# The first MLP product by Strassen's seven block products, and the second in eight banks

## The chip, the cores and the metric

The kernel runs on one core of one Trainium2 chip. The metric is the device time of one execution in microseconds (us), the median over several runs. The engines are named as the profile names them: PE is TensorE (matmuls; PEld its weight loads), DVE VectorE, ACT ScalarE, POOL GpSimd, SP SyncE, which here only issues DMAs. SBUF is the on-chip memory with 128 partitions, PSUM the eight accumulator banks of 512 float32 values per partition, DRAM the memory outside the core.

## The reference

One layer of an encoder on x (512 tokens, 1024 channels, float32). Three branches (a convolution with GLU, differential attention over 8 heads, chunked spatial gating) are projected, gated and summed, and an MLP follows. The MLP is what the change touches:

```python
h = rms_norm(x, norm_ffn_pre[l])
f = jnp.square(jax.nn.relu(h @ w_ffn_up[l]))     # 1024 -> 4096
y = f @ w_ffn_down[l]                            # 4096 -> 1024
x = x + rms_norm(y, norm_ffn_post[l])
```

## The kernel before

All of it is one function, `encoder_layer`. S = 512 is the number of tokens, P = 128 the number of partitions, KT = 8 the channel tiles of the model width, TT = 4 the token tiles, FT = 32 the channel tiles of the MLP's inner width.

**Split products.** Every large matmul runs in float32r. An operand is kept as a high half (a copy on ACT that rounds it) and a low half (a subtraction on DVE), and a product is three matmuls, high by high, high by low, low by high (`mm3`, L227). `unit` (L243) makes one channel tile: 8 contraction tiles by 3, 24 matmuls of 512 moving columns with a 128x128 stationary tile each.

**Weights.** `specs` (L87 to L128) lists all weight blocks of 1024 elements per partition (512 KB) in the order of use. `load_to` (L139) issues a block's DMA on SP into `w_raw`, copies it on ACT to `w_hi` (L150) and subtracts on DVE for `w_lo` (L151); each of the three has three buffers in the pool `wp`, but the last four blocks of the output projection and the MLP's first have their halves in the pool `p4`. `take` (L154) hands out the next blocks and keeps two more under way.

**Order.** A scheduler merges the instructions that the code emits into one order for each engine; PE's matmuls stay in the order of the code. SP, ACT, DVE, PE and POOL each work through their own order, and a buffer that is used again waits for its last reader. A pool that is opened where a closed one lay waits for the readers of that memory in the same way.

**Around the MLP.** The output projection and the second norm (p4, L760 to L814) write x1d to DRAM on SP (L801), and transpose the normed tokens into `h2h` and `h2l` (DVE L224), the MLP's moving operands, held in the pool `hp` in the places of `hh` and `hl`. Since the last tokens come late, the first four channel tiles are begun with their first 256 tokens (L807 to L813) and finished with the second 256 (L819 on): halves of 24 matmuls of 256 columns.

**First product (L817 to L833).** For each of 32 channel tiles 24 matmuls of 512 columns, then Relu (ACT L830), square (DVE L831), high half `fh` (ACT L832) and low half `fl` (DVE L833). Weights are stationary and activations move.

**Second product (L835 to L870).** Here `fh` and `fl` are stationary and the weights move. For each half `nh` of the output's columns, 16 blocks by 4 token tiles by 6 matmuls of 512 into four banks: tag "b" for the first half, "a" for the second. The last 2 or 3 blocks of a half are taken together and done token tile by token tile, with the finish behind each (ACT L860, DVE L861, and for the second half the norm, L869, and the output's DMAs, L870).

Of the kernel before, what the change touches and what calls it, by code (L numbers as in the profile page):

```python
# [40 lines left out]
TURN = {(2, 2): 0, (3, 2): 1, 1: 2, 2: 3}  # L41
W0AT = 1
LOWP = 3000
ZA, ZB, QO, KO, VO, SU, SV, GL = 0, 1024, 2048, 3072, 4096, 5120, 6144, 7168


@with_exitstack
def encoder_layer(ctx: ExitStack, tc: tile.TileContext, a: dict, out: bass.AP):
# [88 lines left out]
    taken = [0]  # L137

    def load_to(n):  # L139
        while len(loaded) < min(n, len(specs)):  # L140
            if len(loaded) in xp["set"] and xp["pool"] is None:
                break
            src = specs[len(loaded)]
            m = src.shape[2]
            raw = wp.tile([P, 1024], F32, tag="raw", bufs=3, name="w_raw")
            p, n_ = (xp["pool"], 5) if len(loaded) in xp["set"] else (wp, 3)
            hi = p.tile([P, 1024], F32R, tag="hi", bufs=n_, name="w_hi")
            lo = p.tile([P, 1024], F32R, tag="lo", bufs=n_, name="w_lo")
            nc.sync.dma_start(raw.rearrange("p (k c) -> p k c", c=m), src)
            act.activation(hi, raw, AF.Copy)  # L150
            vec.tensor_tensor(lo, raw, f32(hi[:, :]), op=ALU.subtract)  # L151
            loaded.append((hi.rearrange("p (k c) -> p k c", c=m), lo.rearrange("p (k c) -> p k c", c=m)))
# [91 lines left out]
        run(unit_gen(b, w, mov))  # L244


    hh = hp.tile([P, KT, S], F32R, tag="hh", name="hh")
    hl = hp.tile([P, KT, S], F32R, tag="hl", name="hl")
    with mk("p0") as p0:
        gpre = p0.tile([P, D], F32, tag="gpre", name="gpre")  # L250
        act.dma_start(gpre, a["norm_mix_pre"].partition_broadcast(P))
# [507 lines left out]

    dp = ctx.enter_context(mk("dp", space=DRAM))  # L760
    x1d = dp.tile([S, D], F32, name="x1d")
    h2h = hp.tile([P, KT, S], F32R, tag="hh", name="h2h")
    h2l = hp.tile([P, KT, S], F32R, tag="hl", name="h2l")
    with mk("p4") as p4:
        xp["pool"] = p4
        gpost = bcast(p4, "gpost", a["norm_mix_post"], D)
# [49 lines left out]

    fp = ctx.enter_context(mk("fp"))  # L817
    gpo = bcast(fp, "gpo", a["norm_ffn_post"], D)
    fh = fp.tile([P, FT, S], F32R, tag="fh", name="fh")  # L819
    fl = fp.tile([P, FT, S], F32R, tag="fl", name="fl")  # L820
    for n in range(FT):
        if n < len(early):
            b = eb[n]
            run(unit_gen(b[:, 256:512], early[n], h2, slice(256, 512)))
        else:
            (w,) = take(1)
            b = bank("a")
            unit(b, w, h2)
        r = fp.tile([P, S], F32, tag="r", bufs=2, name="r")
        act.activation(r, b, AF.Relu)  # L830
        vec.tensor_tensor(r, r, r, op=ALU.mult)  # L831
        act.activation(fh[:, n], r, AF.Copy)  # L832
        vec.tensor_tensor(fl[:, n], r, f32(fh[:, n]), op=ALU.subtract)  # L833

    def down_mm(bs, t, i, w):  # L835
        tk = slice(t * P, (t + 1) * P)
        for k in range(2):
            kt = 2 * i + k
            mm3(bs[t], (fh[:, kt, tk], fl[:, kt, tk]), [x_[:, k] for x_ in w], kt == 0, kt == FT - 1)

    xs = hp.tile([P, TT, D], F32, tag="hh", name="xs")
    us = hp.tile([P, TT, D], F32, tag="hl", name="us")
    pool.dma_start(xs, x1d.rearrange("(t p) c -> p t c", p=P))
    ss = cp.tile([P, TT, 2], F32, tag="fss", name="fss")
    NCH = FT // 2
    es = []
    for nh in range(2):
        bs = [bank("b" if nh == 0 else "a") for _ in range(TT)]
        hf = slice(nh * 512, (nh + 1) * 512)
        tail = 2 + nh  # L850
        for i in range(NCH - tail):
            (w,) = take(1)
            for t in range(TT):
                down_mm(bs, t, i, w)
        ws = take(tail, 1)
        for t in range(TT):
            for i in range(tail):
                down_mm(bs, t, NCH - tail + i, ws[i])
            jk = fp.tile([P, S], F32, tag="r", bufs=2, name="jk")
            act.activation(jk, bs[t], AF.Square, accum_out=ss[:, t, nh:nh + 1])  # L860
            vec.tensor_tensor(us[:, t, hf], bs[t], gpo[:, hf], op=ALU.mult)  # L861
            if nh == 0:
                es.append(eps_with(cp, ss[:, t, 0:1], 1.0 / D))
            else:
                r = rstd_of(cp, ss[:, t, 1:2], 1.0 / D, es[t], es[t])
            if nh:
                for e, i in ((nc.sync, 0), (act, 1)):
                    hf = slice(i * 512, (i + 1) * 512)
                    vec.scalar_tensor_tensor(us[:, t, hf], us[:, t, hf], r, xs[:, t, hf], op0=ALU.mult, op1=ALU.add)  # L869
                    e.dma_start(out[t * P:(t + 1) * P, hf], us[:, t, hf])  # L870
    ph.close()


# [29 lines left out]
```

## Time and profile before

| what | value |
|---|---|
| median of 3 runs | 1090.18 us (1090.12 to 1090.3) |
| the profiled execution's own time | 1090.09 us |
| its span, first to last instruction | 1088.0 us |
| mean granted TensorE clock | 0.997 |
| first product's matmuls, from its first tiles' second token halves on | 740.12 to 906.86 us |
| second product's matmuls | 906.86 to 1080.95 us |
| w_raw's blocks by DMA | 176 of 512 KB |

A row of the chain or the timeline reads: start in us, length in us, engine, line, operation, and output <- inputs. In square brackets stands how long the engine sat idle before it and what ended that. In rows that group instructions, the total of busy time is followed by the mean of one in ns. DVE and ACT overlap the end of an instruction with the start of the next, so the time from one start to the next is what one costs in a row of them. The ends of matmuls are modelled; the distance of their starts is not.

### The profile page before, as it was taken

To read this page: it belongs to the slowest core of one execution; us is meant where nothing else is said; L and a number is where in the kernel's file an instruction comes from. 1 tells how busy PE (TensorE), PEld (TensorE's weight loads), DVE (VectorE), ACT (ScalarE), POOL (GpSimd) and SP (SyncE) were. 2 spreads that over 40 slices of the span, in tenths; PEclk is the share of its full clock that TensorE was granted. 3 is DMA by queue.
4 is the path that set the end of the run, shared out by engine and by line. 5 is a ranking of instruction groups with operands and counts; after the bars stand their busy time and mean duration, and the time that the engine had idled before them with its cause. 6 is when DMAs were issued, how large, how long until landed. Compare 5 with 4: busy or idle time off the path is not lost.

```text
span 1088.0 us, 13538 instructions
## 1 busy us (share of the span) xinstructions
PE 1074.6 (99%) x5232; PEld 904.7 (83%) x5232; DVE 706.2 (65%) x1201; ACT 497.6 (46%) x800; POOL 14.0 (1%) x32
## 2 busy tenths in 40 slices
PE   8999999999999999999999999999999999999997
PEld 7989898988878888888888888889888888888886
DVE  6686878978996888997996554485444443223224
ACT  5356677776654832343222863354444443112111
POOL 3000000000000000000000000000000000000000
PEclk9999999999999999999999999999999999999999
DMA  7242332232333333322333132732333334223222
GB/s 223 78 127 68 96 98 78 78 98 78 93 101 97 97 97 97 97 78 80 98 97 102 52 116 97 277 129 78 97 97 97 97 97 174 97 97 96 97 78 78
DMA packets 149439, 111.78 MB, mean 103 GB/s; under 512 B 3957, under 2 KB 130977, under 8 KB 149376
## 3 DMA queue, kind: packets, MB, share of 16 engines
q1 hardware_dynamic: 146368, 101.73, 31.0%
q0 software_dynamic: 2288, 7.63, 2.0%
q10 hardware_dynamic: 720, 1.57, 0.4%
q8 instruction: 41, 0.67, 0.3%
q14 instruction: 22, 0.18, 0.1%
HBM read 102.52 MB, written 4.19 MB: 98 GB/s over the span
## 4 chain that ended last, share of the span: by engine, by line
PE 94%; DVE 2%; ACT 2%; DMA 1%; SPq 0%; issue 0%; DVEq 0%; ACTq 0%
PE ps_a L57 74%; PE ps_b L57 17%; PE ps_b L61 3%; DMA w_raw<-in_w_in_dram 1%; ACT y L731 0%; DVE jk L805 0%; DVE w_lo L151 0%; PE ps_a L61 0%; SPq L267 0%; ACT jk L803 0%; ACT w_hi L150 0%; DVE wk L800 0%; DVE st L616 0%; DVE h2l L224 0%; DVE wk L799 0%
## 5 line engine op out<-in xcount | busy, mean ns | idle before, releaser
L150 ACT ACTIVATE w_hi<-w_raw 128x1024 fp32r<-128x1024 f32 x176 | 186.5, 1060 | 387.6 <-PE ps_a L57 292.8
L151 DVE TENSOR_TENSOR w_lo<-w_raw,w_hi 128x1024 fp32r<-128x1024 f32 x176 | 215.1, 1223 | 220.8 <-ACT w_hi L150 220.4
L57 PE MATMUL ps_a<-hh,w_hi 128*128 128x512 f32 (+1 forms) x536 | 206.1, 387 | 0.0
L57 PE MATMUL ps_a<-hh,w_lo 128*128 128x512 f32 (+1 forms) x536 | 203.6, 382 | 0.0
L57 PE MATMUL ps_a<-hl,w_hi 128*128 128x512 f32 (+1 forms) x536 | 203.2, 381 | 0.0
L352 DVE SCALAR_TENSOR_TENSOR acc<-apad,convw,acc 128x512 f32<-128x512 f32 x232 | 173.7, 749 | 5.1
L57 PEld LDWEIGHTS ps_a<-hh,w_lo 128*128 128x128 f32 x536 | 101.0, 189 | 19.6
L57 PEld LDWEIGHTS ps_a<-hl,w_hi 128*128 128x128 f32 x536 | 101.2, 190 | 18.4
L57 PEld LDWEIGHTS ps_a<-hh,w_hi 128*128 128x128 f32 x536 | 101.1, 189 | 18.3
L57 PE MATMUL ps_a<-h2h,w_hi 128*128 128x512 f32 (+1 forms) x288 | 105.4, 366 | 0.0
L57 PE MATMUL ps_a<-h2l,w_hi 128*128 128x512 f32 (+1 forms) x288 | 105.3, 366 | 0.0
L57 PE MATMUL ps_a<-h2h,w_lo 128*128 128x512 f32 (+1 forms) x288 | 105.2, 365 | 0.0
L57 PEld LDWEIGHTS ps_a<-h2h,w_hi 128*128 128x128 f32 x288 | 54.3, 189 | 8.8
L57 PEld LDWEIGHTS ps_a<-h2h,w_lo 128*128 128x128 f32 x288 | 54.3, 189 | 8.8
L57 PEld LDWEIGHTS ps_a<-h2l,w_hi 128*128 128x128 f32 x288 | 54.3, 189 | 8.7 <-DVE h2l L224 0.2
L57 PE MATMUL ps_b<-w_hi,fh 128*128 128x512 f32 x128 | 49.8, 389 | 0.0
L57 PE MATMUL ps_b<-w_lo,fh 128*128 128x512 f32 x128 | 49.8, 389 | 0.0
L57 PE MATMUL ps_b<-w_hi,fl 128*128 128x512 f32 x128 | 49.8, 389 | 0.0
L57 PE MATMUL ps_a<-w_hi,fh 128*128 128x512 f32 x128 | 49.8, 389 | 0.0
L57 PE MATMUL ps_a<-w_lo,fh 128*128 128x512 f32 x128 | 49.8, 389 | 0.0
L57 PE MATMUL ps_a<-w_hi,fl 128*128 128x512 f32 x128 | 49.8, 389 | 0.0
L57 PE MATMUL ps_a<-w_hi,hh 128*128 128x256 f32 (+1 forms) x160 | 49.7, 311 | 0.0
(243 smaller groups left out, 1821.9 us busy)
## 6 DMA issues: line engine op xcount, KB each, us to landing
w_raw<-in_w_in_dram SPq DMA_DIRECT2D x80, 512.0 KB, 3.6
w_raw<-in_w_ffn_up_dram SPq DMA_DIRECT2D x32, 512.0 KB, 3.9
w_raw<-in_w_ffn_down_dram SPq DMA_DIRECT2D x32, 512.0 KB, 3.5
w_raw<-in_w_proj_attn_dram SPq DMA_DIRECT2D x8, 512.0 KB, 4.0
w_raw<-in_w_proj_sgu_dram SPq DMA_DIRECT2D x8, 512.0 KB, 3.9
w_raw<-in_w_proj_conv_dram SPq DMA_DIRECT2D x8, 512.0 KB, 4.0
w_raw<-in_w_out_dram SPq DMA_DIRECT2D x8, 512.0 KB, 3.5
xx<-in_x_dram SPq DMA_DIRECT2D x4, 512.0 KB, 7.6
```

Of the source, the lines that this page charges most:

```text
L57: return tc.keep_in_program_order(nc.tensor.matmul(*args, **kw))
L61: return tc.keep_in_program_order(nc.tensor.transpose(*args, **kw))
L150: act.activation(hi, raw, AF.Copy)
L151: vec.tensor_tensor(lo, raw, f32(hi[:, :]), op=ALU.subtract)
L352: vec.scalar_tensor_tensor(o, apad[:, c, j:j + S], convw[:, c, j:j + 1], acc, op0=ALU.mult, op1=ALU.add)
```

## The change

**First product.** The first four channel tiles stay as they are, but f is kept whole: Relu and Square, both on ACT. The other 28 tiles are done as seven groups `q` of 512 channels. Within a group the product of the weights (two halves of 512 contraction rows by two halves of 256 channels: blocks 11, 12, 21, 22) and the activations (two halves of contraction by two of tokens) is made by the Winograd form of Strassen's scheme: seven products, i = 0 to 6, of 24 matmuls with 256 columns. Of their weight operands three are blocks and four are sums of blocks that DVE makes for each group (`operand`); four of the moving operands are sums of activation blocks (`T`), made once ahead of and in the first group (`side`, `block`, `parts`) and kept split in `ring`. The results are combined from PSUM by copies on ACT (`snap`) and sums on DVE (`plus`), some by going on accumulating in a bank. `load_block` issues a group's four weight blocks on SP; block 12 uses `w_raw`'s old buffers, the others six buffers in the pool `fp`, which lies where p4 lay.

**Second product.** f is split while the product runs (`f_part`, two channel tiles at a time, four places in `ring`), and both column halves go along together in eight banks `b0` and `b1`, up to the last three blocks of each. The matmuls are the same 768.

**Places in memory.** `h2h`, `h2l` and the `ring` places of the T operands lie 112 elements further on; a pad shrinks; the small tiles of lam move from pool `cq` to `ap_`, a pool that is opened later.

On DVE, at the start of the MLP, before (h2l is the last of the norm, L831 and L833 the square and low half of f, w_lo a weight's low half):

```order
L805 SCALAR_TENSOR_TENSOR jk<-wk,rs_r,gpre_6225 128x1024
L224 TENSOR_TENSOR h2l<-ps_b,h2h 128x4x128 x2
L831 TENSOR_TENSOR r<-r 128x512
L833 TENSOR_TENSOR fl<-r,fh 128x512
L151 TENSOR_TENSOR w_lo<-w_raw,w_hi 128x1024
L831 TENSOR_TENSOR r<-r 128x512
L151 TENSOR_TENSOR w_lo<-w_raw,w_hi 128x1024
L833 TENSOR_TENSOR fl<-r,fh 128x512
```

And on DVE at the same place now (lines of the changed file: L878 a block sum of activations, L891 to L899 the T sums, L883 their low halves, L931 a weight operand's low half, L920 to L926 the sums of weight blocks, L950 a sum from PSUM):

```order
L931 TENSOR_TENSOR w_lo<-w_raw,w_hi 128x1024
L894 SCALAR_TENSOR_TENSOR f<-f 128x1024
L883 TENSOR_TENSOR ring<-f,ring 128x1024
L931 TENSOR_TENSOR w_lo<-w_raw,w_hi 128x1024
L920 TENSOR_TENSOR w_sum<-w_raw 128x1024
L883 TENSOR_TENSOR ring<-f,ring 128x1024
L878 TENSOR_TENSOR f<-h2h,h2l 128x1024
L931 TENSOR_TENSOR w_lo<-w_sum,w_hi 128x1024
L897 SCALAR_TENSOR_TENSOR f<-f 128x1024
L922 TENSOR_TENSOR w_sum<-w_sum,w_raw 128x1024
L950 TENSOR_TENSOR r<-ps_b,snap 128x512
L883 TENSOR_TENSOR ring<-f,ring 128x1024
```

Ahead of these twelve stand L878 three times and L891; behind them up to the fifth product's low half stand L931, L899, L924, L926, L883 and L931. Where two steps of 512 and one of 1024 stood for a channel tile, the first group has 21 steps of 1024 and one of 512 ahead of its fifth product.

On SP, the DMA issues from the output projection on, now (L156 the old loader, L909 `load_block`, L817 the write of x1d; before, the seven first and the 25 other blocks of the first product stood on either side of x1d):

```order
L156 DMA w_raw<-in_w_out_dram 128x2x512 x8
L156 DMA w_raw<-in_w_ffn_up_dram 128x8x128 x4
L909 DMA w_raw<-in_w_ffn_up_dram 128x4x256
L817 DMA x1d<-wk 128x1024 x4
L909 DMA w_raw<-in_w_ffn_up_dram 128x4x256 x27
L156 DMA w_raw<-in_w_ffn_down_dram 128x2x512 x32
```

Only one block of the first group, 12, is issued ahead of x1d now, and its other three behind.

The diff, without what repeats:

```diff
+SHIFT = 112
...
-    for n in range(FT):
+    PLAIN = 4
+    for n in range(PLAIN):
         specs += [cols("w_ffn_up", n * P)]
-    for nh in range(2):
-        specs += [rows("w_ffn_down", k, nh * 512) for k in range(0, FT, 2)]
+    gate_at = [len(specs)]
+    NCH = FT // 2
+    TAIL = 3
+    down = [(i, nh) for i in range(NCH - TAIL) for nh in range(2)]
+    down += [(i, nh) for nh in range(2) for i in range(NCH - TAIL, NCH)]
+    for i, nh in down:
+        specs += [rows("w_ffn_down", 2 * i, nh * 512)]
...
-        while len(loaded) < min(n, len(specs)):
+        while len(loaded) < min(n, gate_at[0]):
...
+    def held(name, tag, dt, at=0):
+        return hp.tile([P, KT * S + P], dt, tag=tag, name=name)[:, at:at + KT * S]
+    def k_of(t):
+        return t.rearrange("p (k s) -> p k s", s=S)
+    hh = k_of(held("hh", "hh", F32R))
+    hl = k_of(held("hl", "hl", F32R))
...
-    pad(big, "pad2", 416)
+    pad(big, "pad2", 160)
...
-        lq = bcast(cq, f"lq{i}", a[f"lam_q{i}"], 64)
-        lk = bcast(cq, f"lk{i}", a[f"lam_k{i}"], 64)
-        pr = cq.tile([P, 64], F32, tag="lpr", name="lpr")
+        lq = bcast(ap_, f"lq{i}", a[f"lam_q{i}"], 64)
+        lk = bcast(ap_, f"lk{i}", a[f"lam_k{i}"], 64)
+        pr = ap_.tile([P, 64], F32, tag="lpr", name="lpr")
...
+    h2h = k_of(held("h2h", "hh", F32R, SHIFT))
+    h2l = k_of(held("h2l", "hl", F32R, SHIFT))
...
-    fh = fp.tile([P, FT, S], F32R, tag="fh", name="fh")
-    fl = fp.tile([P, FT, S], F32R, tag="fl", name="fl")
-    for n in range(FT):
-        if n < len(early):
-            b = eb[n]
-            run(unit_gen(b[:, 256:512], early[n], h2, slice(256, 512)))
-        else:
-            (w,) = take(1)
-            b = bank("a")
-            unit(b, w, h2)
+    f = fp.tile([P, FT, S], F32, tag="f", name="f")
+    ring = fp.tile([P, 8 * 1024 + P], F32R, tag="ring", name="ring")
+    def half(j, at):
+        return ring[:, at + j * 1024:at + (j + 1) * 1024]
+    def f_out(n, ts, src, sign):
+        act.activation(src, src, AF.Relu, scale=sign)
+        act.activation(f[:, n:n + 2, ts], src.rearrange("p (x t) -> p x t", x=2), AF.Square)
+    for n in range(PLAIN):
+        b = eb[n]
+        run(unit_gen(b[:, 256:512], early[n], h2, slice(256, 512)))
         r = fp.tile([P, S], F32, tag="r", bufs=2, name="r")
         act.activation(r, b, AF.Relu)
-        vec.tensor_tensor(r, r, r, op=ALU.mult)
-        act.activation(fh[:, n], r, AF.Copy)
-        vec.tensor_tensor(fl[:, n], r, f32(fh[:, n]), op=ALU.subtract)
+        act.activation(f[:, n], r, AF.Square)
+    t1, t2 = slice(0, 256), slice(256, 512)
+    def quarter(j, ts):
+        return [t[:, 4 * j:4 * j + 4, ts] for t in h2]
...
+    def block(j, k):
+        h_, l_ = quarter(j, (t1, t2)[k])
+        vec.tensor_tensor(q4(B[j, k]), f32(h_), f32(l_), op=ALU.add)
+    def parts(i):
+        hi, lo = half(2 * i, SHIFT), half(2 * i + 1, SHIFT)
+        act.activation(hi, sums[4 + i], AF.Copy)
+        vec.tensor_tensor(lo, sums[4 + i], f32(hi), op=ALU.subtract)
+        T[i] = q4(hi), q4(lo)
+    def side(i):
+        if i == 0:
+            block(0, 0)
+            block(0, 1)
+            vec.tensor_tensor(sums[4], B[0, 0], B[0, 1], op=ALU.subtract)
+        if i == 1:
+            block(1, 1)
+            vec.scalar_tensor_tensor(sums[5], sums[4], -1.0, B[1, 1], op0=ALU.mult, op1=ALU.subtract)
+        if i == 2:
+            block(1, 0)
+            vec.scalar_tensor_tensor(sums[6], sums[5], -1.0, B[1, 0], op0=ALU.mult, op1=ALU.subtract)
+        if i == 3:
+            vec.tensor_tensor(sums[7], B[1, 1], B[0, 1], op=ALU.subtract)
+        parts(i)
+    blocks = {}
+    def load_block(q, name):
+        if q < FT // 4:
+            i, j = int(name[0]) - 1, int(name[1]) - 1
+            p, tag, n_ = (wp, "raw", 3) if name == "12" else (fp, "aq", 6)
+            t = p.tile([P, 1024], F32, tag=tag, bufs=n_, name="w_raw")
+            nc.sync.dma_start(t.rearrange("p (k c) -> p k c", c=256),
+                              rows4("w_ffn_up", 4 * j, q * 512 + i * 256))
+            blocks[q, name] = t
+    def operand(q, i):
+        if q >= FT // 4:
+            return
+        g = lambda n: blocks[q, n]
+        if i == 2:
+            blocks[q, "x"] = wp.tile([P, 1024], F32, tag="raw", bufs=3, name="w_sum")
+            vec.tensor_tensor(g("x"), g("21"), g("22"), op=ALU.add)
+        if i == 3:
+            vec.tensor_tensor(g("x"), g("x"), g("11"), op=ALU.add)
+        if i == 4:
+            vec.tensor_tensor(g("x"), g("x"), g("12"), op=ALU.add)
+        if i == 6:
+            vec.tensor_tensor(g("21"), g("21"), g("11"), op=ALU.add)
+        raw = g(("11", "12", "x", "x", "x", "22", "21")[i])
+        hi = wp.tile([P, 1024], F32R, tag="hi", bufs=3, name="w_hi")
+        lo = wp.tile([P, 1024], F32R, tag="lo", bufs=3, name="w_lo")
+        act.activation(hi, raw, AF.Copy)
+        vec.tensor_tensor(lo, raw, f32(hi), op=ALU.subtract)
+        blocks[q, i] = [t.rearrange("p (k c) -> p k c", c=256) for t in (hi, lo)]
+    def product(o, q, i, m, first):
+        w = blocks.pop((q, i))
+        for kt in range(4):
+            for x_ in range(2):
+                xc, oc = slice(x_ * P, (x_ + 1) * P), slice(x_ * 256, (x_ + 1) * 256)
+                for p_, (sw, sm) in enumerate(((0, 0), (0, 1), (1, 0))):
+                    pe.matmul(o[:, oc], w[sw][:, kt, xc], m[sm][:, kt], start=first and kt + x_ + p_ == 0,
+                              stop=kt == 3 and p_ == 2, skip_group_check=True)
...
+    def plus(ps_, t):
+        r = fp.tile([P, S], F32, tag="r", bufs=2, name="r")
+        vec.tensor_tensor(r, ps_, t, op=ALU.add)
+        return r
+    for n in ("11", "21", "22", "12"):
+        load_block(1, n)
+    operand(1, 0)
+    operand(1, 1)
+    side(0)
+    for q in range(1, FT // 4):
+        c1, c2 = 4 * q, 4 * q + 2
+        if q == FT // 4 - 1:
+            gate_at[0] = len(specs)
+        def ahead(i):
+            if i + 2 < 7:
+                operand(q, i + 2)
+            elif q + 1 < FT // 4:
+                operand(q + 1, i + 2 - 7)
+            else:
+                load_to(taken[0] + i + 2 - 6)
+            if q == 1 and i in (0, 2, 3):
+                side({0: 1, 2: 2, 3: 3}[i])
+        ahead(0)
+        ba = bank("a")
+        product(ba, q, 0, quarter(0, t1), True)
+        s1 = snap(ba)
+        ahead(1)
+        bd = bank("b")
+        product(bd, q, 1, quarter(1, t1), True)
+        f_out(c1, t1, plus(bd, s1), 1.0)
+        ahead(2)
+        load_block(q + 1, "11")
+        load_block(q + 1, "21")
+        be = bank("a")
+        product(be, q, 2, T[0], True)
+        se = snap(be)
+        ahead(3)
+        product(ba, q, 3, T[1], False)
+        sv = snap(ba)
+        load_block(q + 1, "22")
+        load_block(q + 1, "12")
+        ahead(4)
+        product(be, q, 4, quarter(1, t2), False)
+        f_out(c1, t2, plus(be, sv), 1.0)
+        ahead(5)
+        bc = bank("b")
+        product(bc, q, 5, T[2], True)
+        sc = snap(bc)
+        ahead(6)
+        product(ba, q, 6, T[3], False)
+        f_out(c2, t1, plus(ba, sc), -1.0)
+        f_out(c2, t2, plus(ba, se), -1.0)
+    fparts = {}
+    def f_part(i):
+        if i < NCH:
+            src = f[:, 2 * i:2 * i + 2].rearrange("p n s -> p (n s)")
+            hi, lo = half(2 * (i % 4), 0), half(2 * (i % 4) + 1, 0)
+            act.activation(hi, src, AF.Copy)
+            vec.tensor_tensor(lo, src, f32(hi), op=ALU.subtract)
+            fparts[i] = [t.rearrange("p (k s) -> p k s", s=S) for t in (hi, lo)]
...
+    f_part(0)
...
+    b0 = [bank("a"), bank("a"), bank("b"), bank("b")]
+    b1 = [bank("a"), bank("a"), bank("b"), bank("b")]
...
+    for i in range(NCH - TAIL):
+        f_part(i + 1)
+        for bs in (b0, b1):
             (w,) = take(1)
             for t in range(TT):
                 down_mm(bs, t, i, w)
-        ws = take(tail, 1)
+    for i in range(NCH - TAIL, NCH):
+        f_part(i + 1)
+        (w,) = take(1)
         for t in range(TT):
-            for i in range(tail):
-                down_mm(bs, t, NCH - tail + i, ws[i])
...
+            down_mm(b0, t, i, w)
+    for t in range(TT):
+        finish(0, t, b0)
+    ws = take(TAIL, 0)
+    for t in range(TT):
+        for i in range(TAIL):
+            down_mm(b1, t, NCH - TAIL + i, ws[i])
+        finish(1, t, b1)
```

More of the change, by code (lines that the diff above doesn't have):

```diff
@@ L244, in unit @@
         run(unit_gen(b, w, mov))
-    hh = hp.tile([P, KT, S], F32R, tag="hh", name="hh")
-    hl = hp.tile([P, KT, S], F32R, tag="hl", name="hl")
+    def held(name, tag, dt, at=0):
[4 more added lines that the diff above has]
+    hl = k_of(held("hl", "hl", F32R))
     with mk("p0") as p0:
@@ L761, in encoder_layer @@
     x1d = dp.tile([S, D], F32, name="x1d")
-    h2h = hp.tile([P, KT, S], F32R, tag="hh", name="h2h")
-    h2l = hp.tile([P, KT, S], F32R, tag="hl", name="h2l")
+    h2h = k_of(held("h2h", "hh", F32R, SHIFT))
+    h2l = k_of(held("h2l", "hl", F32R, SHIFT))
     with mk("p4") as p4:
@@ L832, in encoder_layer, with q4 @@
-        act.activation(fh[:, n], r, AF.Copy)
-        vec.tensor_tensor(fl[:, n], r, f32(fh[:, n]), op=ALU.subtract)
+        act.activation(f[:, n], r, AF.Square)
+    t1, t2 = slice(0, 256), slice(256, 512)
+    def quarter(j, ts):
+        return [t[:, 4 * j:4 * j + 4, ts] for t in h2]
+    sums = []
+    for i in range(8):
+        sums.append(f[:, 16 + 2 * i:18 + 2 * i].rearrange("p n s -> p (n s)"))
+    def q4(t):
+        return t.rearrange("p (k s) -> p k s", s=256)
+    B = {}
+    for i, (j, k) in enumerate(((0, 0), (0, 1), (1, 1), (1, 0))):
+        h_, l_ = quarter(j, (t1, t2)[k])
+        B[j, k] = sums[i]
@@ new lines, in encoder_layer @@
+    T = {}
+    def block(j, k):
+        h_, l_ = quarter(j, (t1, t2)[k])
+        vec.tensor_tensor(q4(B[j, k]), f32(h_), f32(l_), op=ALU.add)
[18 more added lines that the diff above has]
+        parts(i)
@@ new lines, in product, with snap @@
+    def product(o, q, i, m, first):
[6 more added lines that the diff above has]
+                              stop=kt == 3 and p_ == 2, skip_group_check=True)
+    def snap(src):
+        t = fp.tile([P, S], F32, tag="sn", bufs=4, name="snap")
+        act.activation(t, src, AF.Copy)
+        return t
@@ L838, in down_mm, with finish @@
             kt = 2 * i + k
-            mm3(bs[t], (fh[:, kt, tk], fl[:, kt, tk]), [x_[:, k] for x_ in w], kt == 0, kt == FT - 1)
-    xs = hp.tile([P, TT, D], F32, tag="hh", name="xs")
-    us = hp.tile([P, TT, D], F32, tag="hl", name="us")
+            mm3(bs[t], [t_[:, k, tk] for t_ in fparts[i]], [x_[:, k] for x_ in w], kt == 0, kt == FT - 1)
+    f_part(0)
+    xs = held("xs", "hh", F32).rearrange("p (t c) -> p t c", c=D)
+    us = held("us", "hl", F32).rearrange("p (t c) -> p t c", c=D)
     pool.dma_start(xs, x1d.rearrange("(t p) c -> p t c", p=P))
     ss = cp.tile([P, TT, 2], F32, tag="fss", name="fss")
-    NCH = FT // 2
     es = []
-    for nh in range(2):
-        bs = [bank("b" if nh == 0 else "a") for _ in range(TT)]
+    b0 = [bank("a"), bank("a"), bank("b"), bank("b")]
+    b1 = [bank("a"), bank("a"), bank("b"), bank("b")]
+    def finish(nh, t, bs):
         hf = slice(nh * 512, (nh + 1) * 512)
-        tail = 2 + nh
-        for i in range(NCH - tail):
+        jk = fp.tile([P, S], F32, tag="r", bufs=2, name="jk")
+        act.activation(jk, bs[t], AF.Square, accum_out=ss[:, t, nh:nh + 1])
+        vec.tensor_tensor(us[:, t, hf], bs[t], gpo[:, hf], op=ALU.mult)
+        if nh == 0:
+            es.append(eps_with(cp, ss[:, t, 0:1], 1.0 / D))
+            return
+        r = rstd_of(cp, ss[:, t, 1:2], 1.0 / D, es[t], es[t])
+        for e, i in ((nc.sync, 0), (act, 1)):
+            hf = slice(i * 512, (i + 1) * 512)
+            vec.scalar_tensor_tensor(us[:, t, hf], us[:, t, hf], r, xs[:, t, hf], op0=ALU.mult, op1=ALU.add)
+            e.dma_start(out[t * P:(t + 1) * P, hf], us[:, t, hf])
+    for i in range(NCH - TAIL):
+        f_part(i + 1)
+        for bs in (b0, b1):
             (w,) = take(1)
@@ L854, in encoder_layer @@
                 down_mm(bs, t, i, w)
-        ws = take(tail, 1)
+    for i in range(NCH - TAIL, NCH):
+        f_part(i + 1)
+        (w,) = take(1)
         for t in range(TT):
-            for i in range(tail):
-                down_mm(bs, t, NCH - tail + i, ws[i])
[L859 to L870, printed above, removed]
+            down_mm(b0, t, i, w)
[6 more added lines that the diff above has]
+        finish(1, t, b1)
     ph.close()
```

## Prediction

> **What bounds it now.** I read the page first, then the chain of waits, then PE's waits. The page:
>
> ```profile
> span 1088.0 us, 13538 instructions
> PE 1074.6 (99%) x5232; PEld 904.7 (83%) x5232; DVE 706.2 (65%) x1201; ACT 497.6 (46%) x800; POOL 14.0 (1%) x32
> PE 94%; DVE 2%; ACT 2%; DMA 1%; SPq 0%; issue 0%; DVEq 0%; ACTq 0%
> ```
>
> PE is 94% of the chain that ended last. The chain in order of time (start, us, what) has the whole MLP as three unbroken pieces of PE, and an attention row that serves as a yardstick:
>
> ```profile
> 20.84 4.37 PE ps_a L57 x24
> ...
> 86.84 2.88 PE ps_a L57 x24
> ...
> 740.12 166.73 PE ps_a L57 x792
> 906.86 87.04 PE ps_b L57 x384
> 993.90 87.05 PE ps_a L57 x384
> 1081.69 0.69 DVE us L861
> ```
>
> From 740.12 to 1080.9 PE never waits, so time comes out of the MLP only by giving PE less to do, and anything that makes PE wait there is paid in full. PE's longest waits all lie ahead of it; two of them:
>
> ```profile
> PE ps_b L61 <- DVE hs L283: 2.6, 1, 2.6
> PE ps_b L57 <- DVE kk L445: 0.5, 1, 0.5
> ```
>
> **PE's pace at both widths.** PE's own rows in the first MLP stretch, each pair 24 matmuls apart (256 columns, then 512):
>
> ```profile
> 742.83 0.28 PE L57 MATMUL ps_a<-h2h,w_hi 128*128 128x256 f32 x1
> ...
> 745.71 0.28 PE L57 MATMUL ps_a<-h2h,w_hi 128*128 128x256 f32 x1
> 780.22 0.39 PE L57 MATMUL ps_a<-h2h,w_hi 128*128 128x512 f32 x1
> ...
> 785.65 0.39 PE L57 MATMUL ps_a<-h2h,w_hi 128*128 128x512 f32 x1
> ```
>
> 2.88/24 = 0.120 us per matmul of 256 columns, 5.43/24 = 0.2263 us per matmul of 512. Half width costs 0.53 of the full width, not half.
>
> **The Strassen products.** Four channel tiles (512 channels) are 4 x 24 = 96 matmuls of 512 before: 21.72 us. After they are 7 products of 24 matmuls of 256: 168 x 0.120 = 20.16 us. Seven such groups save 7 x 1.56 = **10.9 us**. Seven eighths of the columns come out as 0.93 of the time.
>
> The Trainium skill, "TensorE: Matmul & The Clock Gate", section "Back-to-back issue gap", gives one isolated matmul N/2.4 + 2.5 ns, 109.2 and 215.8 ns here; by it the saving would be 7 x (20.72 - 18.35) = 16.6 us. The trace disagrees at both widths, 120 and 226 ns.
>
> **What the other engines must do beside it.** Rows of busy time by window (window, length, PE, PEld, DVE, ACT, POOL, granted clock, DMA):
>
> ```profile
> 84.00:96.00 12.00, 12.00 (x99) 11.78 (x98) 8.31 (x17) 8.10 (x16) 0.00 (x0) 1.00 0.15 44
> 740.00:752.00 12.00, 12.00 (x103) 12.00 (x102) 4.50 (x6) 4.04 (x7) 0.00 (x0) 1.00 0.01 1
> 800.00:850.00 50.00, 50.00 (x222) 41.42 (x221) 23.46 (x29) 19.81 (x28) 0.00 (x0) 1.00 0.33 95
> 17.61:21.03 3.42, 1.26 (x11) 1.29 (x12) 3.25 (x9) 1.80 (x4) 0.00 (x0) 1.00 0.60 194
> 21.03:24.44 3.41, 3.41 (x19) 3.41 (x18) 3.34 (x11) 2.19 (x5) 0.00 (x0) 0.50 0.47 151
> ```
>
> VectorE's rows, from start to start, price its steps:
>
> ```profile
> 731.83 1.28 DVE L805 SCALAR_TENSOR_TENSOR jk<-wk,rs_r,gpre 128x1024 f32<-128x1024 f32 x1
> 733.02 1.28 DVE L800 SCALAR_TENSOR_TENSOR wk<-wk,rs_r,xr 128x1024 f32<-128x1024 f32 x1
> ...
> 740.36 1.29 DVE L224 TENSOR_TENSOR h2l<-ps_b,h2h 128x512 fp32r<-128x512 f32 x2 [1.44 <-ACT h2h L223]
> ...
> 749.76 1.23 DVE L151 TENSOR_TENSOR w_lo<-w_raw,w_hi 128x1024 fp32r<-128x1024 f32 x1 [1.14 <-ACT w_hi L150]
> 750.90 0.69 DVE L831 TENSOR_TENSOR r<-r 128x512 f32<-128x512 f32 x1
> ...
> 753.78 0.69 DVE L833 TENSOR_TENSOR fl<-r,fh 128x512 fp32r<-128x512 f32 x1
> 754.38 0.69 DVE L831 TENSOR_TENSOR r<-r 128x512 f32<-128x512 f32 x1
> ```
>
> So 1.14 us for a tensor_tensor of 1024, 0.60 for one of 512, 1.19 for a scalar_tensor_tensor of 1024. ScalarE's:
>
> ```profile
> 745.91 0.60 ACT L830 ACTIVATE r<-ps_a 128x512 f32<-128x512 f32 x1 [5.10 <-PE ps_a L57]
> ...
> 748.67 1.06 ACT L150 ACTIVATE w_hi<-w_raw 128x1024 fp32r<-128x1024 f32 x1 [0.77 <-PE ps_a L57]
> 749.63 0.58 ACT L830 ACTIVATE r<-ps_a 128x512 f32<-128x512 f32 x1
> ...
> 752.51 0.61 ACT L832 ACTIVATE fh<-r 128x512 fp32r<-128x512 f32 x1
> 753.03 0.58 ACT L830 ACTIVATE r<-ps_a 128x512 f32<-128x512 f32 x1
> ```
>
> 0.96 us for 1024, 0.52 for 512. A settled group gives VectorE 7 low halves, 4 operand sums (1024 each) and 4 PSUM sums (512): 11 x 1.14 + 4 x 0.60 = 14.9 us; ScalarE 7 x 0.96 + 12 x 0.52 = 13.0 us. Both fit into 20.16 us. The tightest operand is the fifth product's: from the end of the second product VectorE has a PSUM sum, two operand sums and a low half, 0.60 + 2 x 1.14 + 1.23 = 4.1 us, while PE has the third and fourth, 2 x 2.88 = 5.76. Settled groups wait **0**, with about 1.6 us to spare.
>
> **The first group** is different: VectorE also makes 4 block sums, 4 sums of these and 4 low halves, and none can start before h2's last low half, which ends at 741.65 (740.36 + 1.29). Three block sums and a subtraction take it to 746.2. Next in its new order stands the low half of block 11, and that block is late: its buffer lies over p4's weight halves, which PE reads last for tile 0's second token half, so its DMA starts at 745.9 (ScalarE's L830 starts on the same event). Landing times, of the old tiles (512 KB each), of all weight tiles, and of the four x tiles that queue together (us, min/median/max):
>
> ```profile
> w_raw<-in_w_ffn_up_dram SPq DMA_DIRECT2D x32, 512.0 KB, 3.9
> DMA to landing us min/median/max: 3.3/3.8/12.3
> DMA to landing us min/median/max: 5.3/7.6/8.7
> ```
>
> I take 3.9: landed at 749.8, high half by 750.9, where the low half starts. From there up to the fifth product's low half VectorE's order has 15 tensor_tensors of 1024, 2 scalar_tensor_tensors and a PSUM sum: 15 x 1.14 + 2 x 1.19 + 0.60 = 20.1, so 771.1 with the last one's 0.09 of drain. PE starts the products at 745.71 + 3 x 2.88 = 754.35 (three more second halves), is through four at 765.87 and needs the low half two matmuls later, at 766.1. So PE waits **5.0 us**: 2.1 before the fourth product (10 + 2 + 1 steps, ready 765.4, wanted 763.2) and 2.9 before the fifth. Ends: 4.4 with the landing at 3.3, 6.4 at 5.3, and 7.7 if a later one of the seven blocks queued on SP is last instead.
>
> **The second product** keeps its 768 matmuls of 512. Splitting f on the fly adds one 1024 copy and one subtraction to each pair of chunks, so VectorE has 3 x 1.14 = 3.4 us of work in 48 x 0.2263 = 10.9: hidden. At its end the third tail weight can only be copied when the first four banks' last matmul has freed a high half, and ScalarE has a Square of the finish ahead of it:
>
> ```profile
> 1080.55 0.39 PE L57 MATMUL ps_a<-w_hi,fl 128*128 128x512 f32 x1
> ...
> 1080.97 0.60 ACT L860 ACTIVATE jk<-ps_a 128x512 f32<-128x512 f32 x1 [2.99 <-PE ps_a L57]
> ```
>
> 0.70 + 1.06 + 1.23 and two handovers of 0.1 make 3.2 us; PE needs it 12 matmuls and one later, 2.95. **+0.25**, between 0 (tile done earlier) and 0.45.
>
> **Edits with one answer.** f whole saves VectorE two of its three steps per tile; it was idle half of 800 to 850, so 0. Relu and Square on ScalarE are counted above. gpo's DMA is issued some 50 us later on POOL and first needed at the first finish, over 200 us on: 0. The three lam pairs of steps, moved to another pool, load behind apad's memsets and come later on VectorE; PE's program order before the MLP is unchanged and its 0.5 us wait lies there: 0, bounds -0.5 (that wait gone) and +1.0 (twice that lost again). The moved address of h2, and that of the ring, show in no row; I take 0, with the pace's price under the rivals as its bound.
>
> **The sum**, against the profiled execution's span: 1088.0 - 10.9 + 5.0 + 0.25 + 0 = 1082.35. That run took 1090.09, 2.09 outside its span, and the median of three is 1090.18, 0.09 above it: 1082.35 + 2.09 + 0.09 = **1084.5 us**.
>
> **Rivals.**
>
> *The clock drops in the first group.* Between 17.61 and 21.03 PE was busy for 1.26 of 3.42 us, and the next 3.41 us ran at a granted clock of 0.50: 24 matmuls took 4.37 us there instead of 2.88. A wait of 2.1 us, a product, and 2.9 us come near that. Half the clock for 3.41 us costs 1.7: 1086.2. Against it: PE is busy between the two waits. The Trainium skill, "TensorE: Matmul & The Clock Gate", Part 1 on the HAM clock gate, has the clock halved after an idle window of about 3.4 us, by which both waits would be too short; the row of 17.61 to 21.03 shows a drop after a window in which PE was 37% busy, so the chance goes by the row.
>
> *The first group hardly waits.* If block 11's buffer is free earlier, the low half starts at 746.2 and not at 750.9, the 5.0 becomes 0.3: 1079.8. For it: only the buffer holds it. Against: the pool's place is fixed before anything runs.
>
> *The pace of the isolated matmul*, 10.9 replaced by 16.6: 1078.8. Both PE pairs speak against it.
>
> *Every group waits.* Should VectorE's 4.1 us for the fifth product grow past 6.0 (5.76 and two matmuls), by ScalarE's copies standing in the way, seven groups pay: 1 us each makes 1091.5, and 0.5 us 1088.0. For it: VectorE's and ScalarE's busy shares rise to 0.74 and 0.65. Against: 1.6 us of slack.
>
> *Slower: the weight port loses its slack.* At 512 columns PEld is busy 41.42 of 50 us, at 256 it is busy 12.00 of 12.00: each matmul needs a new load and nothing is left to absorb one that is late. Seven eighths of the up product move to that regime, with VectorE and ScalarE reading and writing beside it, and operands at new addresses. 1176 matmuls pay any rise: with the 5.25 of waits, the gain is gone at 0.1248 us each and the kernel 0.2% slower from 0.1267; at 0.130 it takes 1096. For it: a PEld without slack. Against: in 84 to 96 VectorE was busy for 8.31 and ScalarE for 8.10 of 12.00 us, and matmuls of 256 still took 2.88/24.
>
> **How the numbers follow.** A measurement of this kernel can tell about 0.2% (2.2 us) from no change: faster is below 1088.0, slower above 1092.4. Chances: the forecast 0.45, the clock drop 0.20, hardly a wait 0.08, the isolated pace 0.03, waits in every group 0.12, the port 0.12. The forecast's own bounds are 1083.2 (4.4, 0, -0.5) to 1088.4 (7.7, 0.45, +1.0). The range 1079.5 to 1089.0 takes in the first three cases and the milder part of the last two; it leaves out about 0.18. Faster: 0.43 + 0.20 + 0.08 + 0.03, half of the group waits and a quarter of the port, 0.83; slower: half of the port and a third of the group waits, 0.10; same 0.07.
>
> **What would show it.** Right: 256-column matmuls 0.120 us apart throughout; one or two waits of PE on VectorE's L931 near 763 to 771, none in later groups; a piece of 768 matmuls without a break of over half a microsecond; a first block landing near 750. Wrong: matmuls over 0.122 us apart in a settled group; the same wait repeated every 20 us; a PE wait for a block's DMA; a granted clock of 0.50 after 766; or a gap ahead of 740 that was not there.

## The result and the profile after

The changed kernel takes 1077.47 us in the median of four executions (1074.89 to 1081.47), the kernel before 1090.24 us: ratio 0.9884, 95% interval 0.9845 to 0.9922. The forecast was 1084.5 us, with a range of 1079.5 to 1089.0: the direction was right and the gain more than twice as large. The profiled execution took 1075.01 us. From its page:

```profile
span 1072.9 us, 14691 instructions
...
PE 1054.8 (98%) x5736; PEld 909.6 (85%) x5736; DVE 770.5 (72%) x1242; ACT 550.2 (51%) x868; POOL 14.1 (1%) x32
...
PE 91%; DVE 4%; ACT 2%; DMA 1%; issue 1%; SPq 0%; DVEq 0%; ACTq 0%
```

PE is still the bound, but 4% of the chain is VectorE now. PE's waits by what ended them (total, times, longest) name it:

```profile
PE ps_a L58 <- DVE w_lo L931: 3.5, 3, 1.8
...
PE ps_a L58 <- ACT w_hi L930: 1.1, 2, 0.6
```

All of L930 and L931 lies in the first group. The chain through the MLP:

```profile
738.32 5.47 PE ps_a L58 x48
743.79 0.02 issue
743.81 3.84 DMA w_raw<-in_w_ffn_up_dram
...
767.53 1.23 DVE w_lo L931
768.77 0.04 issue
768.81 2.78 PE ps_a L58 x22
771.59 2.72 PE ps_b L58 x24
774.31 5.44 PE ps_a L58 x48
...
1046.33 2.73 PE ps_b L58 x12
...
1052.09 5.51 PE ps_a L58 x23
```

2.72/24 = 0.1133 us per matmul of 256 columns, where the kernel before and the forecast had 0.120, and 2.72/12 = 0.2267 for 512 as before (the second product's operands were not shifted against each other). No settled group waits. Against the kernel before, by these rows:

| stretch | forecast | measured | from |
|---|---|---|---|
| start up to the MLP | 0 | -1.8 | 740.12 to 738.32 |
| plain tiles' halves in the MLP (one first, four second) | 0 | -0.8 | 120 x (0.120 - 0.1133) |
| seven groups | -10.9 | -18.8 | 7 x (21.72 - 168 x 0.1133) |
| wait in the first group | +5.0 | +5.75 | 768.81 less 743.79 + 7 x 2.72 + 2 x 0.1133 |
| end of the second product | +0.25 | +0.3 | 1052.09 less 1046.33 + 2.73 + 2.72 |
| sum | -5.65 | -15.35 | spans: 1088.0 - 1072.9 = 15.1 |

So the start and all that runs at the pace of 256 columns went wrong, and both are worked out below. The sum is that of the profiled execution, near the fastest; the four lie up to 6.6 us apart, where those of before lie 1.3 here and at most 3.6 in the larger sets of the later runs.

### The profile page after: what moved, and what is told of

Same layout as the page of the kernel before. It is cut to its first block, busy times and chain, and to the rows that moved or that the text cites. A ratio compares the mean times of both kernels' runs of the same rounds, so it can differ in the third digit from the quotient of the medians.

```text
span 1072.9 us, 14691 instructions
## 1 busy us (share of the span) xinstructions
PE 1054.8 (98%) x5736; PEld 909.6 (85%) x5736; DVE 770.5 (72%) x1242; ACT 550.2 (51%) x868; POOL 14.1 (1%) x32
## 4 chain that ended last, share of the span: by engine, by line
PE 91%; DVE 4%; ACT 2%; DMA 1%; issue 1%; SPq 0%; DVEq 0%; ACTq 0%
PE ps_a L58 68%; PE ps_b L58 20%; PE ps_b L62 3%; DMA w_raw<-in_w_in_dram 1%; DVE w_lo L158 0%; DVE w_lo L931 0%; ACT y L745 0%; ACT w_hi L157 0%; DMA w_raw<-in_w_ffn_up_dram 0%; DVE jk L821 0%; PE ps_a L62 0%; ACT jk L819 0%; SPq L281 0%; DVE hs L297 0%; DVE wk L816 0%
## 5 line engine op out<-in xcount | busy, mean ns | idle before, releaser
L58 PE MATMUL ps_a<-w_hi,ring 128*128 128x512 f32 x256 | 83.7, 389 | 0.0
L58 PE MATMUL ps_b<-w_hi,ring 128*128 128x512 f32 x256 | 83.7, 389 | 0.0
L58 PE MATMUL ps_a<-ring,w_hi 128*128 128x256 f32 x336 | 58.2, 277 | 0.6 <-ACT w_hi L930 0.6
L58 PEld LDWEIGHTS ps_a<-w_hi,ring 128*128 128x128 f32 x256 | 48.1, 188 | 9.9
L58 PEld LDWEIGHTS ps_a<-ring,w_hi 128*128 128x128 f32 x336 | 50.6, 188 | 0.8 <-ACT w_hi L930 0.8
L58 PE MATMUL ps_a<-h2h,w_lo 128*128 128x256 f32 x176 | 48.7, 277 | 1.8 <-DVE w_lo L931 1.8
L58 PE MATMUL ps_a<-w_lo,ring 128*128 128x512 f32 x128 | 49.9, 390 | 0.1
L58 PE MATMUL ps_b<-w_lo,ring 128*128 128x512 f32 x128 | 49.8, 389 | 0.0
L58 PE MATMUL ps_a<-h2h,w_hi 128*128 128x256 f32 x176 | 48.9, 278 | 0.5 <-ACT w_hi L930 0.5
L58 PE MATMUL ps_a<-h2l,w_hi 128*128 128x256 f32 x176 | 48.8, 277 | 0.0
```

The lines of the kernel that those rows point to most:

```text
L58: return tc.keep_in_program_order(nc.tensor.matmul(*args, **kw))
```

## The experiments

**The changed kernel once more**, no edit, beside the next three.

> The changed kernel as it is, once more, to see how far its times lie apart and to have a second profile. If the spread of 1074.9 to 1081.5 us comes from the first group (late blocks, DMA landing), a slower execution shows more than the 4.6 us of PE waits on L930 and L931 there and everything else alike. If it comes from the clock, a slower execution shows stretches of 3.4 us at a granted clock of 0.50, 1.7 us each. If it comes from the pace, the matmuls of 256 columns stand more than 0.1133 us apart over long stretches.

1076.3 us (1076.11 to 1079.88), ratio 0.9877 (0.986 to 0.9893). Its profile shows the same waits, and one thing more. Windows cut where its granted clock changes, and the same stretch of the first profile (busy PE, PEld, DVE, ACT, POOL, granted clock, DMA, GB/s):

```profile
764.66:768.07 3.41, 1.47 (x11) 1.07 (x9) 3.41 (x4) 3.34 (x5) 0.00 (x0) 1.00 0.15 32
768.07:771.48 3.41, 2.95 (x14) 2.95 (x15) 3.41 (x4) 0.47 (x1) 0.00 (x0) 0.50 0.54 168
...
764.64:768.05 3.41, 1.86 (x14) 1.44 (x12) 3.41 (x4) 3.34 (x5) 0.00 (x0) 1.00 0.10 18
```

The clock was halved behind 3.41 us in which PE was busy for 1.47, which costs 0.5 x 3.41 = 1.7 us; in the first profile PE was busy for 1.86 us there, and the clock stayed. Ten of the traces have such a half clock in the middle of the kernel: in nine of them PE had been busy for 1.13 to 1.60 of the 3.41 us before it, in the tenth for 1.81. So the first rival of the prediction is real, in some executions. It can't make 4 to 6 us.

**The addresses moved back.**

```diff
-SHIFT = 112
+SHIFT = 0
```

> The changed kernel with the addresses of h2 and of the T operands moved back by 112 elements, and nothing else. If the place of the moving operand against the stationary one set the pace (my theory), the matmuls of 256 columns go back from 0.1133 to 0.120 us, 1368 of them (1176 in the groups, 192 in the early halves) cost 9.1 us more, and the kernel takes about 1084 us where the changed one takes 1075. If the faster pace comes from something else in the change (the half-bank outputs, the order of the two column tiles), the pace stays 0.1133 and the time the same.

1083.76 us (1083.61 to 1085.09), ratio 0.994 (0.9926 to 0.9953), and the pace of the groups in the chain is that of before, 5.76/48 = 0.120:

```profile
738.35 5.76 PE ps_a L58 x48
...
768.99 4.11 PE ps_a L58 x22
...
776.25 5.76 PE ps_a L58 x48
```

So the 112 elements make the pace. The time lies 0.7 us from the forecast's 1084.5, but this closeness is in part luck: by these rows the MLP starts 1.8 us earlier than before, PE waits for 4.5 us in the first group and not 5.0 (768.99 less 744.11, where the 48 matmuls from 738.35 on end, + 7 x 2.88 + 0.24), and a clock drop (4.11 for 22 matmuls) costs 1.7.

**The pace by itself.** Bursts of 48 matmuls behind the end of the changed kernel, stationary and moving operand in one idle tile.

```diff
+    def burst(cols, at, sat=0):
+        o = bank("a")
+        for j in range(48):
+            s0, m0 = 4096 + sat + j % 8 * P, at + j % 4 * 512
+            pe.matmul(o[:, 0:cols], ring[:, s0:s0 + P], ring[:, m0:m0 + cols], start=True, stop=True)
+    for at in (0, 8, 16, 32, 48, 64, 80, 96, 112, 120):
+        burst(256, at)
+    burst(256, 112, 112)
...
```

> The changed kernel with bursts of 48 matmuls added behind its end, that only read one tile, with the moving operand's address ahead of the stationary one's by 0, 32, 64, 128, 192, 256, 320, 384, 448 and 480 bytes modulo 512, then with both moved by 448, then 512, 128 and 192 columns at 0 and at 448. If the distance of the two addresses counts (my theory), 256 columns take 0.120 us at 0 and 0.1133 at 448, and 0.120 again with both moved. If the absolute place counts, both moved takes 0.1133 too. 512 columns take 0.2267 at both places by the matmuls of the second product.

Windows of equal length inside five bursts (0, 448 and both moved at 256 columns; 0 and 448 at 512) show it by the count of matmuls:

```profile
1070.40:1075.40 5.00, 5.00 (x44) 5.00 (x44) 2.83 (x8) 0.98 (x3) 0.00 (x0) 1.00 0.48 184
...
1115.80:1120.80 5.00, 5.00 (x46) 5.00 (x45) 0.00 (x0) 0.00 (x0) 0.00 (x0) 1.00 0.00 0
1126.90:1131.90 5.00, 5.00 (x44) 5.00 (x43) 0.00 (x0) 0.00 (x0) 0.00 (x0) 1.00 0.00 0
1132.60:1142.60 10.00, 10.00 (x46) 8.24 (x45) 0.00 (x0) 0.00 (x0) 0.00 (x0) 1.00 0.00 0
1143.50:1153.50 10.00, 10.00 (x45) 8.01 (x44) 0.00 (x0) 0.00 (x0) 0.00 (x0) 1.00 0.01 2
```

From start to start, means over the last 43 matmuls of each burst, in ns:

| distance, bytes | 0 | 32 | 64 | 128 | 192 | 256 | 320 | 384 | 448 | 480 | both at 448 |
|---|---|---|---|---|---|---|---|---|---|---|---|
| 256 columns | 120.0 | 117.7 | 117.8 | 118.7 | 113.5 | 119.9 | 117.8 | 118.7 | 113.4 | 118.3 | 120.0 |

With both operands moved the pace is that of distance 0: the distance counts, not the place. The surprise is 512 columns: 227.3 ns at 0 and 233.3 at 448. There the shift costs. 128 and 192 columns take 111.7 ns at either distance; no burst with a fresh stationary tile for each matmul went below that.

**The moves in memory alone**, put into the kernel before (h2 moved, lam in the later pool, smaller pad).

```diff
+    h2h = k_of(held("h2h", "hh", F32R, 112))
+    h2l = k_of(held("h2l", "hl", F32R, 112))
-        lq = bcast(cq, f"lq{i}", a[f"lam_q{i}"], 64)
+        lq = bcast(ap_, f"lq{i}", a[f"lam_q{i}"], 64)
...
```

> The kernel before with the change's moves in memory alone: h2 112 elements further on, lam's tiles in the later pool, the smaller pad. No Strassen, no eight banks. The bursts gave 0.2272 us for 512 columns with the operands 0 apart and 0.2335 at 448 bytes, and 0.120 and 0.1133 for 256. If that holds in the kernel, its 672 matmuls of 512 columns in the first product cost 672 x 0.0065 = 4.3 us more, its 192 of 256 columns 1.3 us less, the start up to the MLP some 1.3 us less (lam): about 1.7 us slower than before, with a first product of 0.233 us per matmul of 512. If the address counted only at 256 columns, the kernel is 2.6 us faster than before.

1092.28 us (1091.88 to 1092.57), ratio 1.0017 (1.0008 to 1.0026): a little slower, as the bursts said. Its first product took 170.41 us instead of 166.73, and its MLP began 1.7 us earlier:

```profile
738.39 170.41 PE ps_a L57 x792
908.81 87.06 PE ps_b L57 x384
```

So the early gain comes with the moves in memory, and since the run with the addresses back has it too, not with the 112 elements. And the same address that speeds Strassen's matmuls up slows whole tiles of 512 down. By itself it is no improvement.

**The same places, other distances.** Bursts as above from 144 to 240 bytes at 256 columns, and from 0 to 256 at 512.

> Bursts of 48 matmuls behind the changed kernel's end, moving operand ahead of the stationary one by 144, 160, 176, 192, 208, 224 and 240 bytes at 256 columns, by 0, 32, 64, 128, 192, 224 and 256 at 512 columns, and by 0 and 192 at 384. If the period is 256 bytes, 192 stands in for 448: 0.1133 there, a window of some tens of bytes around it, back to 0.118 at 144 and 240; 512 columns are slowest (0.2335) at 192 and 0.2272 at 0 and 256.

At 512 columns 227.2 ns at 0, 226.7 at 256, and 228.9 to 233.4 between: the period of 256 bytes holds. 384 columns took 173.6 at 0 and 173.3 at 192. At 256 columns my expectation failed: 192 bytes gave 117.8 ns where the first sweep had 113.5, and none of the seven went below 116.7. The same distance has more than one pace.

**Another profile of the changed kernel.**

> The changed kernel once more, for another profile and two more times: if this execution is one of the slow ones (about 1080), the view of PE's waits names what the 4 us are; the theories are a late block in the first group, a block or ring place late in a later group, or the output's end.

1076.83 us (1076.76 to 1081.24). The profile is of the 1081.24, and its chain shows where its time is:

```profile
768.71 4.39 PE ps_a L58 x22
773.10 2.83 PE ps_b L58 x24
775.93 5.65 PE ps_a L58 x48
```

The waits ahead are those of the faster profile. But from the restart on, all groups run at 0.1178 us instead of 0.1133 (2.83/24, 5.65/48), to the last of them: 7 x 168 - 96 = 1080 matmuls x 0.0045 = 4.9 us, and a clock drop (4.39 for 22) costs 1.7: together 6.6 us above the first profile, where 6.2 were measured. That is the third theory of the first expectation, the pace.

**New starts.** Bursts with the same addresses, each but the first behind a wait for a ScalarE copy that grows from burst to burst.

```diff
+    for at, cols, k in [(112, 256, k) for k in range(16)] + [(0, 256, k) for k in range(0, 16, 4)]:
+        for j in range(48):
...
+        act.activation(r[:, 0:64 + 12 * k], o[:, 0:64 + 12 * k], AF.Copy)
```

> Bursts of 48 matmuls of 256 columns behind the changed kernel's end, all reading the same places: 16 bursts with the operands 448 bytes apart and 4 at 0, each after a wait for a copy on ScalarE whose length grows from burst to burst. If the pace at 448 is chosen by the moment at which PE starts again, some of the 16 run at 0.1133 and others at 0.1178, each throughout, and all four at 0 run at 0.120. If the pace follows from the addresses alone, all 16 are alike.

Of the 16 bursts at 448 bytes 13 ran at 113.3 to 113.4 ns and three, the first, the fifth and the eighth, at 117.8, each to its end; the four at 0 ran at 119.8 to 120.0. The chain's rows of the fourth, fifth and eighth burst and of one at distance 0 (each row takes in the end of its last matmul):

```profile
1083.79 5.75 PE ps_a L58 x48
...
1089.92 5.93 PE ps_a L58 x48
...
1108.55 5.93 PE ps_a L58 x48
...
1170.99 6.02 PE ps_a L58 x48
```

So at this distance a stream of PE can start at either of two paces, and it keeps the one that it starts with. What chooses between them is not shown: behind the first, the bursts at 448 bytes differ in the length of the wait alone.

**The blocks loaded earlier** (the pool's places reordered, loads issued first), in two forms. The first form put f over p4's last weight halves.

```diff
+    for n in ("11", "21", "22", "12"):
+        load_block(1, n)
     f = fp.tile([P, FT, S], F32, tag="f", name="f")
```

> The group's weight blocks get a place that was free long before (over the output projection's operands), and are loaded some 9 us earlier; the block and T sums get places that no late reader holds. If the first group's wait is the late block 11 (my theory), VectorE's chain starts at about 744.4 instead of 748.8, PE's waits there fall from 4.6 to 0.2 to 0.6 us, and the kernel gains 4 us. If VectorE's chain alone is too long (the rival), the waits fall by no more than half. If the spread between executions comes from the late DMAs, it shrinks to that of the kernel before, about 0.2 us.

1074.59 us (1074.53 to 1080.56), ratio 0.987 (0.9848 to 0.9893). PE's waits on L930 and L931 (here L934 and L935), 4.6 us in the first profile, fell to 2.9, not to 0.6. The block was there, but the wait went to the block sums, which now stood where p4's halves are read until 743.8:

```profile
743.78 3.50 DVE L893 TENSOR_TENSOR f<-h2h,h2l 128x1024 f32<-128x1024 f32 x3 [3.98 <-PE ps_a L58]
```

That was a fault of the edit, and the second form mended it (two places of the blocks' pool skipped, so that they lie over jk).

> Again the group's blocks in a place that is free early, but now with f, the sums and the ring where the change has them, so that no step of VectorE waits for tile 0's second half: blocks 11, 21 and 22 lie over jk, last read at 738.3. If the late block is the cause of the first group's wait (my theory), the first low half comes at about 744.4 instead of 748.8 and PE waits 0 to 1.3 us in the group: 4.5 us faster than the changed kernel beside it, 1071.5. If VectorE's own chain is the cause, the wait only shrinks by part, as it did not shrink in the run before, where the wait moved to the block sums. If late DMAs make the spread, it goes with them.

1080.5 us (1075.69 to 1080.73), ratio 0.9896 (0.9878 to 0.9913). The profiled execution ran the groups at 0.1178, and four of the five lie 3.5 to 5.0 us above the fifth. PE's waits there came to 4.2 us, and my theory of the wait fell: the sums ran at 739.75 again, yet the first low half started at 748.10, only 0.67 us earlier than in the changed kernel.

```profile
746.52 0.60 ACT L868 ACTIVATE r<-ps_a 128x512 f32<-128x512 f32 x1 [1.46 <-PE ps_a L58]
747.02 1.05 ACT L936 ACTIVATE w_hi<-w_raw 128x1024 fp32r<-128x1024 f32 x1
```

Behind the block stands the next late thing: ScalarE makes the block's high half only behind tile 1's Relu, when tile 1's second half, the reader of the weight buffer that it takes, ends at 746.5. VectorE idles for 3.7 us all the same.

**The first group's order written out**, so that VectorE makes sums in that time (`issue_after` puts an instruction behind another in its engine's order).

```diff
+    plain(0, last[0][0])
+    plain(1, last[1][0])
+    with tc.issue_after(last[1][0].ins), tc.issue_after(last[1][1].ins):
+        operand(1, 0)
+    plain(2, halves[0][0])
...
```

> The first group's order written out: block sums, T0 and T1 and their halves first on VectorE and ScalarE, the Relu of tiles 1 to 3 each behind the copies that the next operand needs, T2 and T3 behind the second product's low half, blocks over jk's place as in the run before. Theory: the first group waits because its first copy stands behind tile 1's Relu and tile 1's weight buffer (746.5) and VectorE idles from 744.4 to 748.8; with sums done in that gap the fifth product's low half is ready at about 761, 2 us before PE wants it, and PE waits under 0.5 us in the group: 5.7 us less, a span of about 1067.2 and 1069.4 us. And if the pace of 0.1133 or 0.1178 us is chosen when PE starts again after such a wait, all executions now keep 0.1133 to 0.114, the pace that every profile shows ahead of the group, and the times lie within 2 us. Rival: the pace is chosen by something else (the start, the chip), and slow executions 5 us above remain.

1073.88 us (1072.3 to 1078.84), ratio 0.984 (0.9826 to 0.9853). PE's wait there is down to 2.7 us (2.1 on w_lo, 0.6 on w_hi), where I expected under 0.5. The paces stay two: the profile is of the 1078.84, with groups at 0.1178, and the other five lie within 1072.3 to 1074.01.

**Some more steps behind the low halves.**

> As the run before, and now the halves of T2, the sums of T3 and the next group's first sum stand behind the low halves of the fourth and fifth products, which they had held up by some 2 us. Theory: PE no longer waits in the first group (at most 0.3 us), so it never starts again there, keeps the 0.1133 to 0.114 us that it has ahead of the group, and every execution lies near 1069.5 us, within some 2 us (the clock at the start). If some executions still run the groups at 0.1178 without a wait ahead of them, the choice does not come from the restart; if waits remain, both paces remain.

1073.03 us (1072.85 to 1077.31), ratio 0.985 (0.9834 to 0.9867). I expected at most 0.3 us of waits; 2.5 remained, 1.4 of them now in the second group (near 784.3). One execution of five lies 4 us above the others, so this told nothing new on what chooses the pace.

**Eight plain tiles, six groups.**

```diff
-    PLAIN = 4
+    PLAIN = 8
...
+            (w,) = take(1)
+            b = bank("a")
+            run(unit_gen(b[:, 0:256], w, h2, slice(0, 256)))
```

> The changed kernel with eight plain tiles instead of four, the four more each in two halves of 256 columns, and Strassen for the other six groups: the sums have 21 us more before the first group needs them. A group done plainly costs 8 x 24 x 0.1135 = 21.8 us instead of 19.04, 2.75 more, and PE's 5.75 us of waits in the first group go. Theory: no wait there, so no new start of PE, so the pace stays at the 0.1133 to 0.114 us of the tiles ahead; all executions lie near 1072 us, within 2 us of each other. Rival: without a wait some executions still change to 0.1178 (5 us slower), and then the restart is not what chooses.

1072.03 us (1071.76 to 1075.99), ratio 0.985 (0.9831 to 0.9869). The long waits are gone, but two of five executions were 4.0 us above the rest, against my expectation. They left no profile; that of a fast one has one piece out of line in its chain, 8.37 instead of 8.16 us, 0.2 us lost at 784.4 behind a copy on ScalarE:

```profile
779.03 8.37 PE ps_a L58 x72
```

**That copy put first.**

```diff
+                with tc.issue_after(snaps[-1].ins) if q == 2 and i == 3 else ExitStack():
```

> As the run before, and ScalarE's copy of the third product's bank now stands ahead of the sixth operand's high half, since the profile before showed PE 0.2 us late at 784.4 behind that copy. The two slow executions there were 4.0 us above the others, and from that place on 6 x 168 - 96 = 912 less a few matmuls at 0.0045 us more make 4.0. Theory: with this last new start gone, no execution changes to 0.1178, and all five lie within 2 us of 1071.6 (the clock drops apart). Rival: slow executions 4 to 6 us above remain with no wait in the profile; then the choice is open.

1071.68 us, all five within 1071.54 to 1071.94, ratio 0.983 (0.9817 to 0.9844): the lowest median, and these five have no spread. Going by their times, 13 of the 37 executions of the changed kernel and its forms ahead of this one were slow ones; at that rate five fast ones in a row come by chance about one time in nine, so that the new starts of PE bring the slow pace is likely, not shown. PE has no wait from 738.32 on to the second product, and one pace:

```profile
738.32 38.10 PE ps_a L58 x336
776.42 2.72 PE ps_b L58 x24
779.14 8.16 PE ps_a L58 x72
```

## Why the prediction was right and wrong

**The step that failed** is the one on the moved address: "The moved address of h2, and that of the ring, show in no row; I take 0, with the pace's price under the rivals as its bound." The term that I took as 0 measured 0.0067 us on 1176 matmuls, 7.9 us, and 0.8 us on the five halves in the MLP. (The other 72 matmuls of the early halves gained nothing: the MLP starts at 738.32 with the shift and at 738.35 without it.) I priced 256 columns from rows in which every pair of operands lay 0 bytes apart modulo 256, and bounded what a new address could do only on the slow side. By the addresses of the built programs, every float32r pair of the kernel before lies 0 apart, and the pairs of 256 columns in the changed MLP lie 448 bytes apart modulo 512, 192 modulo 256. So no row could show the gain; a bound on the fast side, as for any operation that the trace lacks, was what was missing. With the addresses back, the kernel takes 1083.76. That the pace at the new distance has a second value, 0.1178, was not in the forecast either; going by their times, two of the four executions ran at it, and so the median of 1077.47 lies above the fastest 1074.89.

**The lam step** was taken as 0 with bounds of -0.5 and +1.0; the start gave -1.8. In the profile before, lam's four DMAs leave POOL between 5.6 and 10 us, a weight's high half comes late behind its DMA, PE's wait of 2.6 us for L283 follows, and behind that the half clock. In all 14 profiles with lam moved, its DMAs leave from 23 us on, that high half starts at 13.9 to 14.2, and there is no half clock near 21. ScalarE's row before, then after:

```profile
15.28 1.06 ACT L150 ACTIVATE w_hi<-w_raw 128x1024 fp32r<-128x1024 f32 x1 [1.31 <-DMA w_raw<-in_w_in_dram]
...
14.18 1.06 ACT L157 ACTIVATE w_hi<-w_raw 128x1024 fp32r<-128x1024 f32 x1 [0.41 <-DMA w_raw<-in_w_in_dram]
```

No run moves lam alone, so that its DMAs held up the weight's is argued, not shown. I had the row of 4.37 us and its price, and used it only for the rival.

**Right, by size:** the first group's wait (5.0; it was 4.5 at the forecast's pace and 5.75 at the faster one, at which PE arrives earlier), the end (0.25, then 0.3), no wait in settled groups, the second product at its old pace, the 1.7 us of the clock drop where it comes. **Right by number, wrong by cause:** the block's landing at 3.9 (3.84 measured), but its lateness was not what mattered: with it gone the wait stayed.

**The rivals.** "The pace of the isolated matmul" gave 1078.8, near the result by luck, since the mechanism is another: 512 columns stayed at 0.2267. The rival of the weight port did not come: the pace went the other way, down to 0.1133. The first group did wait, no settled group did, and the clock drop came in some executions beside the forecast's wait.

## What to carry to other kernels

Before pricing a matmul at a narrow width from another place in the program, compare the addresses of both operands there with those of the new one, and bound the price to both sides if they differ. A shift that suits 256 columns can harm 512: 0.1133 against 0.120, and 0.2333 against 0.2273. Where times spread in steps, compare the pace behind the last wait of PE; the wait's length was 5.75 us here, and the pace that it left behind could cost 4.9 us more.

## What the runs showed of the hardware

A float32r matmul with fresh weights at 256 columns takes 0.120 us with its operands 0 bytes apart modulo 256, in every burst and kernel measured. At other distances it took 0.113 to 0.119 us, and where one distance was measured again (448 bytes in many streams, 192 in two) there were two paces, 0.1133 to 0.1135 and 0.1178. Why the distance counts was not measured. The Trainium skill, "TensorE: Matmul & The Clock Gate", section "Step-by-step: what each phase is for", says that TensorE has two independent read ports and that loading the next weights takes no bandwidth from the running matmul. By that one would not expect the distance of the two addresses to matter; in the sweep the same loads and matmuls took up to 6% more by the distance alone (120.0 against 113.4 ns), and the measurement decides. The least spacing, 111.7 ns at 128 and 192 columns, lies above the estimate of 128/1.2 = 107 ns that the rule in the same page's section "LDWEIGHTS (loading the stationary operand)" of the Trainium skill gives for a load of 128 columns; the order of size agrees.
